# Two-layer hybrid block (S5, DeltaNet, attention) on one core: convolution taps and weight splits moved from ScalarE and GpSimd to VectorE

## The chip, the cores and the metric

The kernel runs on one core of a Trainium2 chip. A core has TensorE (PE, with its weight loads shown as PEld), VectorE (DVE), ScalarE (ACT), GpSimd (POOL) and SyncE (SP), each working through its own queue of instructions in order; an instruction that waits holds everything behind it in its queue. The metric is the device time of one execution in microseconds (us), the median of a few runs.

## The reference, cut to what matters

Two layers over 512 latent tokens and 256 context tokens, model width 1024. In each layer the modulated, normalised input `h` goes through one input projection whose columns feed three token mixers: the bidirectional S5 scan (`u`), the gated DeltaNet (`dq`, `dk`, `dv`, `dz`), and windowed attention (`aq`, `ak`, `av`), beside the merge gates:

```python
(u, dq, dk, dv, dz, db, da, aq, ak, av, gates) = split_cols(h @ w_in, IN_SPLITS)
...
qkv = jnp.concatenate([q, k, v], axis=-1)
qkv = lax.conv_general_dilated(qkv, conv_w[:, None, :].astype(qkv.dtype), window_strides=(1,),
                               padding=[(DN_CONV // 2, DN_CONV // 2)],
                               dimension_numbers=('NWC', 'WIO', 'NWC'),
                               feature_group_count=qkv.shape[-1])
qkv = jax.nn.silu(qkv.astype(jnp.float32))
```

The convolution is depthwise over tokens with 5 taps (`DN_CONV = 5`) on 1536 channels. The first layer also puts out the context stream; the second does not, so there some work is on the 512 latent tokens alone.

## The kernel before, in words

Features lie on the 128 partitions and tokens along the free dimension. Every projection goes by weight tiles of 128 output features: `load_w` fetches a 128x1024 tile (`ws`, three buffers), ScalarE casts it to a high part `wh` (L230), and the engine `g.wle` subtracts to get the low part `wl` (L231); `wh` and `wl` have two buffers each. PE then multiplies three products of high and low parts (`gemm_h`, L180) into a PSUM tile `pg`, of which there are two. `g.wle` is VectorE, except between L1381 and the lines that set it back (L1472 in the first layer, L1514 in the second), the mixer part of a layer, where it is GpSimd.

For each of the 12 feature tiles of the convolution (`conv`, L1398) the PSUM result is copied by ScalarE into a padded tile `cxp` (L943, L945), whose pads GpSimd clears (L942). ScalarE makes tap 0 into `cac` (L949). A tap `j` of 1 to 4 with `j < dve` is one multiply-and-add on VectorE (L952); any other is a ScalarE multiply into a tile `ctp` (L955) and a GpSimd addition into `cac` (L956). The tables `CDV0` and `CDV1` (L1534, L1535) give `dve` for each tile of the first and second layer. ScalarE's tanh (L957) and four VectorE products (L964) finish the tile in `ctp`, and `put` sends it to memory. `cxp`, `cac` and `ctp` have two buffers each. A tile has 772 columns with context and 512 without; in the second layer tiles 0 to 3 (queries) have 512.

While the convolutions run, VectorE also holds the S5 scan, `s5_in` (L649): a recurrence of many steps of four operations each (`mac`, L706 to L709, 384 columns at first, 64 in its later part), and a tail that adds carried state (L729 to L732, 112 to 448 columns). `s5_out` (L736) reads the state on PE (L755 and L757 in the first layer, L762 and L767 in the second, with tables `gm` loaded from memory).

The second layer's program order is `ORD1`: convolutions 4 to 11, 0 to 3, then the attention's keys and values, its queries, then `dn_ba` (L977, L984), then the S5 read-out, attention heads, gates and the DeltaNet main part. The Tile framework's scheduler orders the instructions of each engine from dependencies and its own model of durations, so an edit of one instruction can move others in every engine's queue.

Of the kernel before, what the change touches and what calls it, by code (L numbers as in the profile page):

```python
# [8 lines left out]
F32 = mybir.dt.float32  # L9
# [3 lines left out]
OP = mybir.AluOpType  # L13
# [203 lines left out]
def load_raw(g, src, n=1):  # L217
    t = g.wp.tile([128, 1024], F32, name="ws", tag="ws", bufs=3)
    with paced(g.ldp, g.tc):
        g.wl_last = g.nc.sync.dma_start(t, src).ins  # L220
    return t


def load_w(g, l, i, pool=None):
    nc = g.nc
    s = load_raw(g, g.A["wt"][l, i])
    pool, bufs = (g.wp, 2) if pool is None else (pool, 6)
    hi = pool.tile([128, 1024], F32R, name="wh", tag="wh", bufs=bufs)
    lo = pool.tile([128, 1024], F32R, name="wl", tag="wl", bufs=bufs)
    nc.scalar.copy(hi, s)  # L230
    g.wle.tensor_tensor(lo, s, hi.bitcast(F32), op=OP.subtract)  # L231
    return hi, lo


# [54 lines left out]
def drain(it, n=1):  # L289
    for _ in range(n):  # L290
        next(it, None)
# [642 lines left out]
CW = TOK + 4  # L934
CPAD = TOK + 8


def dn_conv(g, l, pool, i, pl, pc, out_cb, dve):
    nc = g.nc
    xp = pool.tile([128, CPAD], F32, name="cxp", tag="cxp", bufs=2)  # L940
    for a in (0, 2 + LAT, CPAD - 2):
        nc.gpsimd.memset(xp[:, a:a + (4 if a == 2 + LAT else 2)], 0.0)  # L942
    nc.scalar.copy(xp[:, 2:2 + LAT], pl)  # L943
    if pc is not None:
        nc.scalar.copy(xp[:, 6 + LAT:6 + TOK], pc)  # L945
    w = CW if pc is not None else LAT
    cv = g.sm[:, SM_CV + 60 * l + 5 * i:SM_CV + 60 * l + 5 * i + 5]
    acc = pool.tile([128, CW], F32, name="cac", tag="cac", bufs=2)
    nc.scalar.mul(acc[:, :w], xp[:, 0:w], cv[:, 0:1])  # L949
    for j in range(1, 5):  # L950
        if j < dve:
            nc.vector.scalar_tensor_tensor(acc[:, :w], xp[:, j:j + w], cv[:, j:j + 1], acc[:, :w], op0=OP.mult, op1=OP.add)  # L952
        else:
            tap = pool.tile([128, CW], F32, name="ctp", tag="ctp", bufs=2)
            nc.scalar.mul(tap[:, :w], xp[:, j:j + w], cv[:, j:j + 1])  # L955
            nc.gpsimd.tensor_tensor(acc[:, :w], acc[:, :w], tap[:, :w], op=OP.add)  # L956
    nc.scalar.activation(xp[:, :w], acc[:, :w], AF.Tanh, scale=0.5)  # L957
    n = TOK if pc is not None else LAT
    o = pool.tile([128, CW], F32, name="ctp", tag="ctp", bufs=2)[:, :TOK]
    o3 = o.rearrange("p (c i) -> p c i", i=64)  # L960
    for a, m, dst in ((0, 4, o3[:, 0:8:2]), (256, 4, o3[:, 7::-2]), (LAT + 4, 2, o3[:, 8:12:2]), (LAT + 132, 2, o3[:, 11:8:-2])):
        if a < LAT or pc is not None:
            s_ = lambda t: t[:, a:a + 64 * m].rearrange("p (c i) -> p c i", i=64)
            nc.vector.scalar_tensor_tensor(dst, s_(xp), 1.0, s_(acc), op0=OP.add, op1=OP.mult)  # L964
    out_cb(i, o[:, :n])
# [394 lines left out]
def mixers(g, l, hp):  # L1360
    g.marks = {}
    nc, tc, A = g.nc, g.tc, g.A
# [14 lines left out]
    for m in range(4):  # L1377
        w = load_w(g, l, W_U + m)
        for s in both:
            s5_u(g, p5a, ud, u4, m, gemm_h(g, w, s, tag=UT[l] if s == "c" else "g"), s)  # L1380
    g.wle = nc.gpsimd  # L1381

    def s5_start():
        p5b_ = tc.tile_pool(name=f"s5b{l}", bufs=1, reuse_waits="tile")
# [10 lines left out]
    def put(i, acc):  # L1395
        dma(g, QC).dma_start(cvd[i][:, :acc.shape[1]], acc)

    def conv(i, pc, dve=5):  # L1398
        w = load_w(g, l, W_DQ + i)
        pl = gemm_h(g, w, "l")  # L1400
        pcx = gemm_h(g, w, "c") if (cx or i >= 4) else None
        dn_conv(g, l, pc, i, pl, pcx, put, dve)

    def att_kv():
        w = load_w(g, l, W_AK)
# [35 lines left out]
    if cx:  # L1441
# [7 lines left out]
        with tc.tile_pool(name=f"a1{l}", bufs=1, side="right", reuse_waits="tile") as a1:  # L1449
            att_setup(g, l, pa, pa, a1, cx)  # L1450
            ad = adaln(g, 0, range(4, 12), a1, AD1)
            drain(ad)
            att_kv()
            for x, i in enumerate(list(range(4, 12)) + list(range(4))):
                conv(i, a1, CDV0[x])
                drain(ad)
                if x in HS:
                    with tc.issue_after(g.wl_last) if HI else nullcontext():
                        g.hst.pop(0)()
            bat = dn_ba(g, l, a1)  # L1460
# [8 lines left out]
            drain(so, 17)  # L1469
        pa_.__exit__(None, None, None)  # L1470
        s5_close()
        g.wle = nc.vector  # L1472

        def fill(wh):
            if wh == "out":
                place(g, gt, G0, H0, sum(GU0.values()))
# [4 lines left out]
    else:  # L1481
# [3 lines left out]
        a1 = a1_.__enter__()  # L1485
        p5b_, omi, so = s5_start()
        att_setup(g, l, pa, a1, a1, cx)
        qs, x = [None] * 4, 0
        for e in ORD1.split():
            if e == "kv":  # L1490
                att_kv()
            elif e[0] == "q":
                qs[int(e[1])] = att_qt(int(e[1]))
            else:
                conv(int(e), a1, CDV1[x])
                x += 1
        bat = dn_ba(g, l, a1)
        a1_.__exit__(None, None, None)
# [12 lines left out]
        drain(so)  # L1511
        drain(un, N_PRE)
        s5_close()
        g.wle = nc.vector  # L1514

        def fill(wh):
            if wh == "pair":
                drain(un, N_PAIR)
# [12 lines left out]
T0A = 4  # L1531
AD0 = 7
AD1 = 3
CDV0 = [3, 3, 2, 3, 3, 2, 3, 3, 5, 3, 2, 3]  # L1534
CDV1 = [4, 5, 4, 5, 2, 2, 2, 2, 3, 3, 3, 3]  # L1535
ORD1 = "4 5 6 7 8 9 10 11 0 1 2 3 kv q0 q1 q2 q3"
SO0 = 12
SN0 = 2
# [281 lines left out]
def hybrid_block(ctx, tc, A, out):  # L1820
    nc = tc.nc
    g = Ctx()
    g.tc, g.nc, g.A, g.es = tc, nc, A, ctx
    g.tb, g.hd, g.rside, g.pbs, g.plan, g.ldp, g.hst = {}, {}, "right", [], [], [], []
    g.wle = nc.vector
    setup(g)
    s5a_open(g, 0)
    cond_setup(g)
# [76 lines left out]
```

## Time and profile before

| what | value |
|---|---|
| runs | 2878.09, 2886.13, 2887.59 us; median 2886.13 |
| profiled execution | 2888.32 us, span 2886.6 us |
| PE, DVE, ACT, POOL busy | 92%, 58%, 31%, 21% of the span |

Busy shares are means over a span whose stages have different limits. The convolutions of the first layer lie at about 198 to 344 us and those of the second at about 1808 to 1941 us; the rest of each layer's mixers follows them, and the projections and the MLP of a layer lie behind that.

### The profile page before, as it was taken

The page shows a single profiled execution, that of the slowest core. Times are in us where ns is not written, and L with a number is a line of the kernel's source. Part 1 is how long each engine was busy: PE and PEld are TensorE (multiplying, and loading weights), DVE is VectorE, ACT ScalarE, POOL GpSimd, SP SyncE. Part 2 cuts the span into 40 slices and gives each one's busy share as a digit, 9 for nine tenths or more (in the row PEclk, how much of TensorE's full clock was granted, in tenths as well). Part 3 has the DMA queues.
Part 4 walks back from the last instruction along what each step waited for, and adds up shares of the span by engine and source line. Part 5 has one row for each costly group of instructions (what it writes and reads, how often), then busy time and mean ns, then how long its engine had stood idle before and what let it go on. Part 6 is the DMA issues. An engine that isn't in the chain of part 4 may idle for free.

```text
span 2886.6 us, 45481 instructions
## 1 busy us (share of the span) xinstructions
PE 2669.2 (92%) x17644; PEld 2187.7 (76%) x17644; DVE 1669.0 (58%) x4015; ACT 909.1 (31%) x1641; POOL 612.2 (21%) x774
## 2 busy tenths in 40 slices
PE   4698899999999899999999999759997999999998
PEld 1575688878777788788788878647775768889997
DVE  7859763237335665999933324994466368444443
ACT  2343443133222333213131324333342234323322
POOL 5644521021112311000000011562142133100001
PEclk8799997599999999999999999879998999999999
DMA  7665322224315442576421125124433226222232
GB/s 235 177 204 181 136 77 79 69 103 145 91 41 174 139 152 74 163 229 192 119 68 62 65 90 165 64 82 135 134 116 86 99 84 204 93 95 95 88 103 66
DMA packets 206760, 344.62 MB, mean 119 GB/s; under 512 B 89296, under 2 KB 121168, under 8 KB 206416
## 3 DMA queue, kind: packets, MB, share of 16 engines
q1 hardware_dynamic: 171856, 298.61, 32.6%
q0 software_dynamic: 9600, 36.71, 3.8%
q10 hardware_dynamic: 25088, 6.40, 1.0%
q8 instruction: 139, 2.28, 0.3%
q14 instruction: 77, 0.63, 0.1%
HBM read 270.09 MB, written 68.16 MB: 117 GB/s over the span
## 4 chain that ended last, share of the span: by engine, by line
PE 73%; DVE 14%; issue 4%; DMA 4%; POOL 2%; ACT 2%; SPq 1%; ACTq 0%; DVEq 0%; POOLq 0%
PE pg L180 51%; PE pg L1636 4%; PE ps L757 2%; DVE cac L952 2%; PE ps L917 1%; PE ps L906 1%; PE pm L1259 1%; PE pm L1290 1%; DVE st L709 1%; PE pm L1268 1%; PE pg L1686 1%; PE pm L874 1%; PE ps L1305 1%; DVE wl L231 1%; ACT wh L230 1%
## 5 line engine op out<-in xcount | busy, mean ns | idle before, releaser
L230 ACT CAST wh<-ws 128x1024 fp32r<-128x1024 f32 x272 | 285.1, 1049 | 601.6 <-PE pg L180 465.9
L231 DVE TENSOR_TENSOR wl<-ws,wh 128x1024 fp32r<-128x1024 f32 x234 | 293.6, 1256 | 279.7 <-ACT wh L230 275.5
L180 PE MATMUL pg<-hhil,wh 128*128 128x512 f32 x720 | 296.4, 412 | 39.2 <-ACT cxp L943 38.3
L180 PE MATMUL pg<-hhil,wl 128*128 128x512 f32 x720 | 291.7, 405 | 2.2 <-DVE wl L231 2.2
L180 PE MATMUL pg<-hhi,wh 128*128 128x256 f32 (+1 forms) x800 | 280.1, 350 | 14.7 <-ACT cxp L943 13.4
L180 PE MATMUL pg<-hlol,wh 128*128 128x512 f32 x720 | 293.0, 407 | 0.0
L180 PE MATMUL pg<-hh,wh 128*128 128x512 f32 (+1 forms) x832 | 286.3, 346 | 7.2 <-DVE x L1733 6.5
L180 PE MATMUL pg<-hh,wl 128*128 128x512 f32 (+1 forms) x832 | 285.3, 344 | 1.0 <-DVE wl L231 1.0
L180 PE MATMUL pg<-hl,wh 128*128 128x512 f32 (+1 forms) x832 | 285.2, 343 | 0.5 <-DVE hl L1349 0.5
L180 PE MATMUL pg<-hlo,wh 128*128 128x256 f32 (+1 forms) x800 | 279.0, 349 | 1.7 <-DVE hlo L390 1.7
L180 PE MATMUL pg<-hhi,wl 128*128 128x256 f32 (+1 forms) x800 | 276.9, 346 | 0.0
L180 PEld LDWEIGHTS pg<-hhil,wh 128*128 128x128 f32 x720 | 139.3, 194 | 76.3 <-ACT cxp L943 39.7
L180 PEld LDWEIGHTS pg<-hhi,wh 128*128 128x128 f32 x800 | 152.6, 191 | 44.7 <-ACT cxp L943 16.4
L180 PEld LDWEIGHTS pg<-hh,wh 128*128 128x128 f32 x832 | 157.6, 190 | 29.8 <-DVE x L1733 6.4
L1733 DVE SCALAR_TENSOR_TENSOR x<-pg,modv,x 128x512 f32<-128x512 f32 (+1 forms) x104 | 64.7, 626 | 196.8 <-PE pg L180 196.4
L180 PEld LDWEIGHTS pg<-hh,wl 128*128 128x128 f32 x832 | 157.8, 190 | 25.5 <-issue 4.7
L180 PEld LDWEIGHTS pg<-hlo,wh 128*128 128x128 f32 x800 | 152.7, 191 | 31.4 <-issue 12.6
L180 PEld LDWEIGHTS pg<-hl,wh 128*128 128x128 f32 x832 | 157.8, 190 | 22.2 <-issue 4.1
L180 PEld LDWEIGHTS pg<-hhi,wl 128*128 128x128 f32 x800 | 152.8, 191 | 26.7 <-issue 10.5
L180 PEld LDWEIGHTS pg<-hhil,wl 128*128 128x128 f32 x720 | 138.9, 193 | 38.6 <-issue 4.4
L180 PEld LDWEIGHTS pg<-hlol,wh 128*128 128x128 f32 x720 | 139.5, 194 | 32.2 <-issue 3.1
L231 POOL TENSOR_TENSOR wl<-ws,wh 128x1024 fp32r<-128x1024 f32 x38 | 104.6, 2753 | 119.8 <-ACT wh L230 119.7
(463 smaller groups left out, 6033.2 us busy)
## 6 DMA issues: line engine op xcount, KB each, us to landing
ws<-in_wt SPq DMA_DIRECT2D x272, 512.0 KB, 3.6
wa<-in_wmod SPq DMA_DIRECT2D x48, 512.0 KB, 4.9
wa<-in_wmodt SPq DMA_DIRECT2D x48, 512.0 KB, 4.3
gtd<-gr POOLq DMA_DIRECT2D x24, 384.0 KB, 2.9
tg<-gtd POOLq DMA_DIRECT2D x24, 384.0 KB, 3.4
tb<-tC SPq DMA_DIRECT2D x64, 128.0 KB, 2.8
cvd<-ctp SPq DMA_DIRECT2D x20, 384.0 KB, 2.6
gtd<-gr POOLq DMA_DIRECT2D x24, 256.0 KB, 2.6
```

The costliest lines, as they stand in the source:

```text
L180: g.nc.tensor.matmul(ps, lhsT=wt[:, a], rhs=x(k), start=i == 0, stop=i == n - 1)
L230: nc.scalar.copy(hi, s)
L231: g.wle.tensor_tensor(lo, s, hi.bitcast(F32), op=OP.subtract)
L709: v.tensor_tensor(o, t[0], t[1], op=OP.add)
L757: nc.tensor.matmul(o, lhsT=gm[pp, k * 128:k * 128 + 128], rhs=st[pp, k % 2, k // 2, c0:, pr], start=False, stop=k == 3)
L874: nc.tensor.matmul(o, lhsT=q[:, kv, ns], rhs=a.kh[:, kv, ks], start=True, stop=False)
L906: nc.tensor.transpose(p[:, x * 128:x * 128 + 128], Ps[kv][:, i * 128:i * 128 + 128], g.ident)
L917: mi = nc.tensor.matmul(po[64 * kv:64 * kv + 64, :128], lhsT=a.v[:, kt, 64 * kv:64 * kv + 64], rhs=PT[:, 2 * i + kv, :], start=i == 0, sto ...
L952: nc.vector.scalar_tensor_tensor(acc[:, :w], xp[:, j:j + w], cv[:, j:j + 1], acc[:, :w], op0=OP.mult, op1=OP.add)
L1259: nc.tensor.matmul(pk[pps[d], cx(i)], lhsT=kq(h, 0, ch[d]), rhs=S[x][:, d, i], start=True, stop=True, tile_position=(0, 64 * hd[d]))
L1636: nc.tensor.matmul(ps, lhsT=wt[:, a], rhs=x[:, k, sl], start=i == 0, stop=i == 11)
L1733: g.nc.vector.scalar_tensor_tensor(g.x[:, m, sl], acc, g.modv[:, l, 40 + m, p.r:p.r + 1], g.x[:, m, sl], op0=OP.mult, op1=OP.add)
```

## The change

Every tap 1 to 4 becomes a multiply-and-add on VectorE, so the 47 ScalarE multiplies into `ctp` (L955) and 47 GpSimd additions (L956) are gone; 39 of the taps have 772 columns and 8 have 512. The low part of a weight tile is always made on VectorE, which moves 38 of the subtractions there from GpSimd. No other instruction is added or removed.

```diff
@@ -228,7 +228,7 @@
     hi = pool.tile([128, 1024], F32R, name="wh", tag="wh", bufs=bufs)
     lo = pool.tile([128, 1024], F32R, name="wl", tag="wl", bufs=bufs)
     nc.scalar.copy(hi, s)
-    g.wle.tensor_tensor(lo, s, hi.bitcast(F32), op=OP.subtract)
+    nc.vector.tensor_tensor(lo, s, hi.bitcast(F32), op=OP.subtract)
     return hi, lo
 
 
@@ -935,7 +935,7 @@
 CPAD = TOK + 8
 
 
-def dn_conv(g, l, pool, i, pl, pc, out_cb, dve):
+def dn_conv(g, l, pool, i, pl, pc, out_cb):
     nc = g.nc
     xp = pool.tile([128, CPAD], F32, name="cxp", tag="cxp", bufs=2)
     for a in (0, 2 + LAT, CPAD - 2):
@@ -948,12 +948,7 @@
     acc = pool.tile([128, CW], F32, name="cac", tag="cac", bufs=2)
     nc.scalar.mul(acc[:, :w], xp[:, 0:w], cv[:, 0:1])
     for j in range(1, 5):
-        if j < dve:
-            nc.vector.scalar_tensor_tensor(acc[:, :w], xp[:, j:j + w], cv[:, j:j + 1], acc[:, :w], op0=OP.mult, op1=OP.add)
-        else:
-            tap = pool.tile([128, CW], F32, name="ctp", tag="ctp", bufs=2)
-            nc.scalar.mul(tap[:, :w], xp[:, j:j + w], cv[:, j:j + 1])
-            nc.gpsimd.tensor_tensor(acc[:, :w], acc[:, :w], tap[:, :w], op=OP.add)
+        nc.vector.scalar_tensor_tensor(acc[:, :w], xp[:, j:j + w], cv[:, j:j + 1], acc[:, :w], op0=OP.mult, op1=OP.add)
     nc.scalar.activation(xp[:, :w], acc[:, :w], AF.Tanh, scale=0.5)
     n = TOK if pc is not None else LAT
     o = pool.tile([128, CW], F32, name="ctp", tag="ctp", bufs=2)[:, :TOK]
@@ -1378,7 +1373,6 @@
         w = load_w(g, l, W_U + m)
         for s in both:
             s5_u(g, p5a, ud, u4, m, gemm_h(g, w, s, tag=UT[l] if s == "c" else "g"), s)
-    g.wle = nc.gpsimd
 
     def s5_start():
         p5b_ = tc.tile_pool(name=f"s5b{l}", bufs=1, reuse_waits="tile")
@@ -1395,11 +1389,11 @@
     def put(i, acc):
         dma(g, QC).dma_start(cvd[i][:, :acc.shape[1]], acc)
 
-    def conv(i, pc, dve=5):
+    def conv(i, pc):
         w = load_w(g, l, W_DQ + i)
         pl = gemm_h(g, w, "l")
         pcx = gemm_h(g, w, "c") if (cx or i >= 4) else None
-        dn_conv(g, l, pc, i, pl, pcx, put, dve)
+        dn_conv(g, l, pc, i, pl, pcx, put)
 
     def att_kv():
         w = load_w(g, l, W_AK)
@@ -1452,7 +1446,7 @@
             drain(ad)
             att_kv()
             for x, i in enumerate(list(range(4, 12)) + list(range(4))):
-                conv(i, a1, CDV0[x])
+                conv(i, a1)
                 drain(ad)
                 if x in HS:
                     with tc.issue_after(g.wl_last) if HI else nullcontext():
@@ -1469,8 +1463,7 @@
             drain(so, 17)
         pa_.__exit__(None, None, None)
         s5_close()
-        g.wle = nc.vector
-
+    
         def fill(wh):
             if wh == "out":
                 place(g, gt, G0, H0, sum(GU0.values()))
@@ -1492,7 +1485,7 @@
             elif e[0] == "q":
                 qs[int(e[1])] = att_qt(int(e[1]))
             else:
-                conv(int(e), a1, CDV1[x])
+                conv(int(e), a1)
                 x += 1
         bat = dn_ba(g, l, a1)
         a1_.__exit__(None, None, None)
@@ -1511,8 +1504,7 @@
         drain(so)
         drain(un, N_PRE)
         s5_close()
-        g.wle = nc.vector
-
+    
         def fill(wh):
             if wh == "pair":
                 drain(un, N_PAIR)
@@ -1531,8 +1523,6 @@
 T0A = 4
 AD0 = 7
 AD1 = 3
-CDV0 = [3, 3, 2, 3, 3, 2, 3, 3, 5, 3, 2, 3]
-CDV1 = [4, 5, 4, 5, 2, 2, 2, 2, 3, 3, 3, 3]
 ORD1 = "4 5 6 7 8 9 10 11 0 1 2 3 kv q0 q1 q2 q3"
 SO0 = 12
 SN0 = 2
@@ -1822,7 +1812,6 @@
     g = Ctx()
     g.tc, g.nc, g.A, g.es = tc, nc, A, ctx
     g.tb, g.hd, g.rside, g.pbs, g.plan, g.ldp, g.hst = {}, {}, "right", [], [], [], []
-    g.wle = nc.vector
     setup(g)
     s5a_open(g, 0)
     cond_setup(g)
```

Because the scheduler orders each queue, the edit moves other instructions too. Three places are shown. Rows name the line of the respective file, so L952 of before is L951 of the changed kernel, and L964 is L959.

The first is on DVE in the second layer, at the end of the last convolution. Before:

```order
L732 TENSOR_TENSOR st<-scs 128x3x7x16
L732 TENSOR_TENSOR st<-scr 128x7x16
L952 SCALAR_TENSOR_TENSOR cac<-cxp,sm,cac 128x512
L729 TENSOR_TENSOR scs<-st,apw_16612 128x112
L730 TENSOR_TENSOR scs<-st,apw_16612 128x112
L952 SCALAR_TENSOR_TENSOR cac<-cxp,sm,cac 128x512
L731 TENSOR_TENSOR scs<-scs,st 128x112
L964 SCALAR_TENSOR_TENSOR ctp<-cxp,cac 128x4x64 x2
L732 TENSOR_TENSOR st<-scs 128x7x16
L964 SCALAR_TENSOR_TENSOR ctp<-cxp,cac 128x4x64 x2
L808 STREAM_SHUFFLE ash<-arf 128x512
```

The last rows of the S5 tail (L729 to L732) stand among the last taps, and the last L964 is followed by attention work (L808) alone. In the changed kernel, the same place around the last L959:

```order
L951 SCALAR_TENSOR_TENSOR cac<-cxp,sm,cac 128x512
L708 TENSOR_TENSOR scr<-scr,st 128x64
L951 SCALAR_TENSOR_TENSOR cac<-cxp,sm,cac 128x512
L709 TENSOR_TENSOR st<-scr 128x2x2x16
L231 TENSOR_TENSOR wl<-ws,wh 128x1024
L706 TENSOR_TENSOR scs<-st,apw_16562 128x64
L707 TENSOR_TENSOR scs<-st,apw_16562 128x64
L959 SCALAR_TENSOR_TENSOR ctp<-cxp,cac 128x4x64 x2
L808 STREAM_SHUFFLE ash<-arf 128x512
L708 TENSOR_TENSOR scs<-scs,st 128x64
L810 TENSOR_TENSOR ash<-ash,rt 128x512
L709 TENSOR_TENSOR st<-scs 128x2x2x16
```

Here the 64-column recurrence is still under way at the last convolution's end. The first rows of the S5 tail in the changed kernel come some twenty rows behind that:

```order
L729 TENSOR_TENSOR scr<-st,apw_16562 128x448
L730 TENSOR_TENSOR scr<-st,apw_16562 128x448
L708 TENSOR_TENSOR scs<-scs,st 128x64
L731 TENSOR_TENSOR scr<-scr,st 128x448
L709 TENSOR_TENSOR st<-scs 128x2x2x16
L732 TENSOR_TENSOR st<-scr 128x4x112
```

All 24 operations with 448 columns, 24 with 336 and 8 with 112 of the tail, and 18 operations with 64 columns of the recurrence, stand behind the last L959; before, none stood behind the last L964.

The second place is on PE in the second layer, where the first read-out of the S5 state stands (L767). Before:

```order
L180 MATMUL pg<-hhic,wh 128x256
L180 MATMUL pg<-hloc,wh 128x256
L180 MATMUL pg<-hhic,wl 128x256
L767 MATMUL ps<-gm,st 64x128 x8
L762 MATMUL ps<-mt,u_16357 64x128 x2
L767 MATMUL ps<-gm,st 64x128 x8
L762 MATMUL ps<-mt,u_16357 64x128
L180 MATMUL pg<-hhil,wh 128x512
L180 MATMUL pg<-hlol,wh 128x512
```

L767 comes right behind the context part of the value projection (L180 with 256 columns). In the changed kernel:

```order
L180 MATMUL pg<-hhil,wh 128x512
L180 MATMUL pg<-hlol,wh 128x512
L180 MATMUL pg<-hhil,wl 128x512
L874 MATMUL pm<-akh,aq 128x384
L875 MATMUL pm<-akl,aq 128x384
L874 MATMUL pm<-akh,aq 128x384
L767 MATMUL ps<-gm,st 64x128 x8
L762 MATMUL ps<-mt,u_16307 64x128 x2
L767 MATMUL ps<-gm,st 64x128 x8
L762 MATMUL ps<-mt,u_16307 64x128 x2
L767 MATMUL ps<-gm,st 64x128 x8
```

It now comes behind the four query projections, `dn_ba`, the first gate projections (57 more matmuls of 512 columns of the gates than stood ahead of the DeltaNet main part before) and the first attention products (L874): 537 matmuls of 512 columns of the projections stand between the layer's S5 input (L685) and it, where 312 stood before.

The third is on DVE in the first layer, during the convolutions; before:

```order
L706 TENSOR_TENSOR scs<-st,apw_1338 128x384
L707 TENSOR_TENSOR scs<-st,apw_1338 128x384
L952 SCALAR_TENSOR_TENSOR cac<-cxp,sm,cac 128x772
L709 TENSOR_TENSOR st<-scr 128x2x12x16
L708 TENSOR_TENSOR scs<-scs,st 128x384
L952 SCALAR_TENSOR_TENSOR cac<-cxp,sm,cac 128x772
L706 TENSOR_TENSOR scr<-st,apw_1338 128x384
L707 TENSOR_TENSOR scr<-st,apw_1338 128x384
L262 TENSOR_REDUCE md<-ps 128x8
L709 TENSOR_TENSOR st<-scs 128x2x12x16
```

and in the changed kernel at the same place:

```order
L951 SCALAR_TENSOR_TENSOR cac<-cxp,sm,cac 128x772
L706 TENSOR_TENSOR scs<-st,apw_1338 128x384
L707 TENSOR_TENSOR scs<-st,apw_1338 128x384
L709 TENSOR_TENSOR st<-scr 128x2x12x16
L951 SCALAR_TENSOR_TENSOR cac<-cxp,sm,cac 128x772
L708 TENSOR_TENSOR scs<-scs,st 128x384
L231 TENSOR_TENSOR wl<-ws,wh 128x1024
L706 TENSOR_TENSOR scr<-st,apw_1338 128x384
L707 TENSOR_TENSOR scr<-st,apw_1338 128x384
L709 TENSOR_TENSOR st<-scs 128x2x12x16
L951 SCALAR_TENSOR_TENSOR cac<-cxp,sm,cac 128x772
```

The four taps of a tile, and a weight's low part (L231), now stand in one queue with the recurrence.

## Rows read from the trace of the kernel before

**Rows 1.** The page: busy time, share and instructions of each engine.

```profile
PE 2669.2 (92%) x17644; PEld 2187.7 (76%) x17644; DVE 1669.0 (58%) x4015; ACT 909.1 (31%) x1641; POOL 612.2 (21%) x774
```

**Rows 2.** Windows: start:end length, busy (count) PE PEld DVE ACT POOL, PEclk, DMA, GB/s.

```profile
198.00:328.00 130.00, 112.36 (x587) 76.40 (x584) 128.07 (x221) 48.50 (x68) 69.45 (x50) 0.95 0.52 184
...
1808.00:1943.00 135.00, 87.51 (x386) 71.44 (x385) 130.76 (x206) 49.23 (x66) 81.59 (x55) 0.82 0.20 67
1943.00:2010.00 67.00, 62.52 (x411) 47.75 (x413) 29.95 (x55) 23.01 (x39) 17.93 (x14) 0.92 0.48 143
2010.00:2086.00 76.00, 76.00 (x518) 58.93 (x515) 29.07 (x91) 25.57 (x43) 8.90 (x19) 1.00 0.45 145
2086.00:2222.00 136.00, 122.77 (x1007) 98.11 (x1006) 99.71 (x347) 56.58 (x131) 46.61 (x88) 0.92 0.37 102
```

**Rows 3.** PE's waits in 198 to 345: line, releaser, us, times, longest.

```profile
PE pg L180 <- ACT cxp L943: 13.4, 6, 5.5
```

**Rows 4.** PE's waits in 1808 to 1955.

```profile
PE pg L180 <- ACT cxp L943: 43.4, 6, 13.1
PE ps L767 <- DMA gm<-tb: 8.5, 1, 8.5
```

**Rows 5.** DVE timeline, 211 to 222: start, duration (us).

```profile
214.05 0.55 DVE L708 TENSOR_TENSOR scr<-scr,st 128x384 f32<-128x384 f32 x1
214.51 2.20 DVE L706 TENSOR_TENSOR scs<-st,apw 128x384 f32<-128x384 f32 x1
```

**Rows 6.** POOL timeline, 205 to 222; the last row holds three additions.

```profile
214.27 6.21 POOL L956 TENSOR_TENSOR cac<-cac,ctp 128x772 f32<-128x772 f32 x3 [0.85 <-DVE cac L952]
```

**Rows 7.** DVE timelines, 244 to 252 and 1904 to 1912.

```profile
247.72 1.01 DVE L952 SCALAR_TENSOR_TENSOR cac<-cxp,sm,cac 128x772 f32<-128x772 f32 x1
248.66 0.55 DVE L708 TENSOR_TENSOR scs<-scs,st 128x384 f32<-128x384 f32 x1
...
1907.72 0.74 DVE L952 SCALAR_TENSOR_TENSOR cac<-cxp,sm,cac 128x512 f32<-128x512 f32 x1
```

**Rows 8.** DVE groups by shape, 198 to 328: count, busy us, mean ns, idle before.

```profile
L952 DVE SCALAR_TENSOR_TENSOR cac<-cxp,sm,cac 128x772 f32<-128x772 f32 x17 | 23.6, 1387 | 0.0
L264 DVE TENSOR_TENSOR modv<-md,sm 128x8 f32<-128x8 f32 x7 | 8.2, 1174 | 0.0
```

**Rows 9.** DVE groups by shape, 1808 to 1943.

```profile
L952 DVE SCALAR_TENSOR_TENSOR cac<-cxp,sm,cac 128x772 f32<-128x772 f32 x11 | 15.8, 1440 | 3.6 <-ACT cac L949 3.6
L952 DVE SCALAR_TENSOR_TENSOR cac<-cxp,sm,cac 128x512 f32<-128x512 f32 x8 | 11.2, 1396 | 0.0
...
L732 DVE TENSOR_TENSOR st<-scs 128x448 f32<-128x448 f32 x3 | 1.8, 615 | 0.0
...
L707 DVE TENSOR_TENSOR scs<-st,apw 128x64 f32<-128x64 f32 x6 | 1.3, 217 | 0.0
```

**Rows 10.** POOL groups by shape, 198 to 328.

```profile
L956 POOL TENSOR_TENSOR cac<-cac,ctp 128x772 f32<-128x772 f32 x18 | 43.4, 2409 | 20.0 <-DVE cac L952 14.4 <-ACT wh L230 1.5 <-ACT ctp L955 1.1
L231 POOL TENSOR_TENSOR wl<-ws,wh 128x1024 fp32r<-128x1024 f32 x8 | 25.7, 3207 | 8.3 <-ACT wh L230 8.3
```

**Rows 11.** POOL groups by shape, 1808 to 1943.

```profile
L956 POOL TENSOR_TENSOR cac<-cac,ctp 128x772 f32<-128x772 f32 x13 | 33.6, 2584 | 10.8 <-issue 5.2 <-ACT ctp L955 4.4 <-DVE cac L952 0.9
L231 POOL TENSOR_TENSOR wl<-ws,wh 128x1024 fp32r<-128x1024 f32 x11 | 33.2, 3017 | 16.9 <-ACT wh L230 16.8
L956 POOL TENSOR_TENSOR cac<-cac,ctp 128x512 f32<-128x512 f32 x7 | 14.2, 2026 | 6.7 <-DVE cac L952 4.0 <-ACT ctp L955 2.7
```

**Rows 12.** The page, costliest groups: the weight split on each engine.

```profile
L231 DVE TENSOR_TENSOR wl<-ws,wh 128x1024 fp32r<-128x1024 f32 x234 | 293.6, 1256 | 279.7 <-ACT wh L230 275.5
...
L231 POOL TENSOR_TENSOR wl<-ws,wh 128x1024 fp32r<-128x1024 f32 x38 | 104.6, 2753 | 119.8 <-ACT wh L230 119.7
```

**Rows 13.** PE timeline, 2070 to 2072: start, duration (us).

```profile
2070.14 0.39 PE L180 MATMUL pg<-hlol,wh 128*128 128x512 f32 x1
2070.37 0.39 PE L180 MATMUL pg<-hhil,wl 128*128 128x512 f32 x1
```

## The prediction

> **What bounds the kernel now.** I read the page's busy shares first. PE is busy 92% of the span and DVE 58% [rows 1], so over the whole kernel PE is the bound and little can be gained except where PE starves. The windows by stage say where that is. In the first layer's convolutions, 198 to 328 us, DVE is busy 128.07 of 130 us and PE 112.36; in the second layer's, 1808 to 1943, DVE is busy 130.76 of 135 us and PE only 87.51, at a granted clock of 0.82 [rows 2]. The next two stages are PE's (62.52 of 67 and 76.00 of 76, DVE at 29.95 and 29.07), and the DeltaNet stage from 2086 lies between (PE 122.77 of 136, DVE 99.71) [rows 2]. PE's waits name what is late: its gemms wait for ACT's copy of PSUM into `cxp`, 13.4 us in the first layer and 43.4 us in the second [rows 3, 4]. That copy waits for a `cxp` buffer, which DVE's last products of an earlier tile free. So both stages hang on DVE's queue, and an edit there is worth what it takes from that queue, until PE's own work ends later.
>
> **What DVE's time is made of.** The timeline shows a two-input operation of 128x384 at 0.55 us when alone, and the same shape at 2.20 us while GpSimd runs its additions L956 at 214.27 to 220.48 [rows 5, 6]. A 772-column tap takes 1.01 us alone, a 512-column one 0.74 [rows 7], yet their means in the stages are 1387, 1440 and 1396 ns, and L264, with 8 columns, averages 1174 [rows 8, 9]. I call the excess over the lone duration a stall. For the taps it is 17 x (1.387 - 1.01) = 6.4 us in the first stage, and 11 x 0.43 + 8 x 0.656 = 4.7 + 5.2 = 9.9 us in the second. The same subtraction over every form of the two DVE views gives 44 and 48 us. A check: GpSimd spends 43.4 + 25.7 = 69.1 us of the first stage and 33.6 + 33.2 + 14.2 = 81.0 us of the second in additions and splits [rows 10, 11], so a stall of 44 and 48 is 0.6 of that time, and cannot be more than all of it.
>
> The Trainium skill (SBUF — State Buffer, section Who interferes with whom) says that a DVE instruction with two SBUF inputs and a GpSimd instruction that reads SBUF share one port pair under an exclusive lock, so that the loser fully blocks. Rows 5 and 6 agree as to the pairing; by a full block throughout, the stall would be all of 69.1 and 81.0 us, and the measured excess is less.
>
> **The change, part by part.**
>
> *GpSimd's additions and splits go.* In the two stages nothing of GpSimd is left but memsets of 0.1 us or so. The stalls of 44 and 48 us go with them. Bounds: nothing (if the stretch had another cause) and 69.1 and 81.0 us. I take 44 and 48, worked out from this kernel's own durations.
>
> *DVE gets taps and splits.* Consecutive DVE operations overlap, so a tap costs the distance to the next start: 248.66 - 247.72 = 0.94 us for 772 columns, and with the same 0.07 off, 0.67 for 512 [rows 7]. A split on DVE has a mean of 1256 ns over 234 of them [rows 12]; less the same overlap and some stalls, 1.14. First stage: 18 taps and 8 splits [rows 10], 18 x 0.94 + 8 x 1.14 = 26 us. Second: 13 and 7 taps and 11 splits [rows 11], 12.2 + 4.7 + 12.5 = 29 us. DVE's queue gets shorter by 44 - 26 = 18 and 48 - 29 = 19 us. If every added operation still had its stretched price, about 1.4 us a tap and, in the same ratio, 1.7 a split, the added cost would be 39 and 47, and the net 5 and 1.
>
> *ACT loses 47 multiplies.* ACT is busy 48.50 of 130 and 49.23 of 135 us [rows 2]; that time was never the bound, but a tap no longer passes through two other engines. I cost this at nothing, for DVE's full queue covers it.
>
> *The order on DVE in the second layer.* As the rows of the order show, all of the S5 tail and 18 steps of the recurrence move behind the last convolution's last product. At lone durations this is 24 x 0.615 for 448 columns, 18 x 0.217 for 64 [rows 9], and between them in proportion 24 x 0.50 for 336 and 8 x 0.27 for 112: 32.8 us, less 0.07 of overlap for each of 74 operations: 27.5 us. It is not saved, but put beside the kv, query and gate gemms, where DVE has 37 and 47 us free in 67 and 76 [rows 2]. So the last convolution ends 19 + 27 = 46 us earlier, bounded by PE's floor there: 87.51 x 0.82 = 72 us at full clock against 135 - 46 = 89. PE's 43.4 us of waits [rows 4] are what is bought, with 8.5 of the wait for `gm`, which is late only because the read-out stands early.
>
> *What is given back.* PE's read-out now stands behind 57 more gate matmuls. At the step of PE for 512 columns, 2070.37 - 2070.14 = 0.23 us [rows 13], they make 13.3 us of work that filled before the DeltaNet stage, where PE already idles 136 - 122.77 = 13.2 us [rows 2]. That stage's DVE (99.71 of 136) may then have nothing for PE to do beside it. Between nothing and 13 given back, and as DVE's moved tail also competes with the attention's DVE work, I take 10: second layer 46 - 10 = 36 us.
>
> *First layer.* DVE's 18 us meets PE's floor: PE idles only 130 - 112.36 = 17.6 us there [rows 2], and 13.4 of that is the wait that goes [rows 3]. DVE's need falls to 128 - 18 = 110, PE's stays at 112.4: two near-equal chains that feed each other through two PSUM tiles do not both run full. I take 12, between 0 and 17.6. The order of PE behind the convolutions stays as it was.
>
> Other splits of the 38 lie in the attention stages where DVE has slack, and are costed at nothing; without that cover they would be 19 x 1.14 = 22 us.
>
> **Sum.** 12 + 36 = 48 us from the profiled execution's 2888.3, so 2840; that execution is 2.2 above the median of the runs, so 2838 for the median. Changes under 0.3% (8.7 us) can't be told from none.
>
> **The rivals.**
>
> *Only the stalls count.* If the moved S5 tail makes the read-out, the heads or the DeltaNet stage late by as much as the convolutions gained, 27 is lost: 12 + 19 = 31, or 19 alone if PE holds the first stage. 2855 to 2867. For it: S5's end gates L767, and PE waited for tables there [rows 4]. Against: PE's order has 537 - 312 = 225 more gemm matmuls ahead of that point, which at 0.23 us is 52 us of cover.
>
> *More than that.* If nothing is given back and the first stage gains PE's whole 17.6: 17.6 + 46 = 64, so 2822; and with the granted clock of the DeltaNet stage rising from 0.92 to the 1.00 of the stage before it [rows 2], 122.77 x 0.08 = 10 more: 2812.
>
> *No change.* First layer 0 (PE's floor), second 46 - 27 - 13 = 6: 2880. It needs all give-backs at once.
>
> *Slower: the splits hold DVE's queue.* GpSimd's splits waited 119.7 us in all for ACT's cast [rows 12], a wait that there stopped only later additions. In DVE's in-order queue the recurrence and the taps stand behind the split, as the third place of the order shows; a wait there stops everything. At all of it, 120 - 48 = 72 us slower, 2958; it decides against my forecast from 48 us of such waits. Against: in the two saturated stages it was only 8.3 and 16.8 us [rows 10, 11], and the scheduler puts a split where it expects the cast to be done. DVE's 234 splits show such waits too (279.7 us idle [rows 12]), but in stages with DVE slack.
>
> *Slower: the stretch was not GpSimd's.* Then DVE, busy 98% and 97%, gets 26 + 29 = 55 us more: 2941. Rows 5 and 6 speak against it.
>
> The Trainium skill (Perfetto Trace Analysis, section Optimizing Scalar/DVE Operations) speaks against this change: where DVE is saturated, moving work off it to ScalarE or even GpSimd may make sense, and the change does the reverse. It adds that GpSimd and DVE share an SBUF read port, so that moving work between those two might not help, which rows 5 and 6 bear out.
>
> **Chances.** Forecast (2822 to 2854) 0.66; more than that 0.05; stalls only 0.15; no change 0.06; splits in the queue 0.05; stretch not GpSimd's 0.03. Faster: 0.66 + 0.05 + 0.15 = 0.86 and a little of the no-change case, 0.87; same 0.05; slower 0.08. The range 2812 to 2870 takes in the first three cases.
>
> **What would show it.** In the profile after, two-input DVE operations in the convolution stages should have their lone durations (taps near 1.0 and 0.74, L706 at 0.55 us); PE's wait for `cxp` in the second layer should fall from 43.4 to under 15 us and the clock there rise above 0.82; the last convolution should end near 1941 - 12 - 46 = 1883 us; the tail L729 to L732 should run beside kv and query gemms. It is wrong if DVE shows waits for the cast of tens of us in these stages, if L767 or the heads wait for L732, or if PE's idle time in the DeltaNet stage grows by over 13 us.

## The result and the profile after

The changed kernel takes 2806.76 us (median of 4 runs, 2803.78 to 2808.68), the kernel before 2882.66 (4 runs, 2878.09 to 2887.59): the ratio is 0.974, with a 95% interval of 0.9724 to 0.9756, so 70 to 80 us faster. The forecast was 2838, with a range of 2812 to 2870, so the time lies 5 us below the range. The direction and the mechanism held; the gain of 76 us was sized at 48.

The page's line of busy times, which answers to [rows 1]:

```profile
span 2806.9 us, 45417 instructions
PE 2642.2 (94%) x17644; PEld 2171.5 (77%) x17644; DVE 1643.6 (59%) x4100; ACT 871.0 (31%) x1594; POOL 402.5 (14%) x689
```

The span is 79.7 us shorter (2886.6 - 2806.9). PE runs the same 17644 matmuls, but is busy for 27.0 us less (2669.2 - 2642.2) and idle for 52.7 less. DVE has 85 more instructions, the 47 taps and 38 splits, and yet is busy for 25 us less. This is the first thing to see: more work, less time on the engine that got it.

The DVE groups by shape of the changed kernel, first in 198 to 323 us (first layer's convolutions), then in 1780 to 1868 (second layer's), answer to [rows 8, 9]:

```profile
L951 DVE SCALAR_TENSOR_TENSOR cac<-cxp,sm,cac 128x772 f32<-128x772 f32 x42 | 42.5, 1015 | 0.2 <-issue 0.2
L231 DVE TENSOR_TENSOR wl<-ws,wh 128x1024 fp32r<-128x1024 f32 x10 | 12.2, 1223 | 7.4 <-ACT wh L230 7.3
...
L706 DVE TENSOR_TENSOR scs<-st,apw 128x384 f32<-128x384 f32 x7 | 3.8, 550 | 0.0
...
L951 DVE SCALAR_TENSOR_TENSOR cac<-cxp,sm,cac 128x512 f32<-128x512 f32 x16 | 11.7, 744 | 0.0
```

Taps are at 1015 and 744 ns, where before they averaged 1387 to 1440 and 1396; the recurrence is at 550 ns. These are the lone durations of [rows 5, 7]. The splits' waits for the cast, the fear of one rival, are 7.3 us here and 2.5 in the second layer.

Windows over the same two stages and two later ones (columns as in [rows 2]):

```profile
198.00:323.00 125.00, 123.56 (x706) 87.29 (x705) 111.39 (x239) 42.51 (x61) 1.54 (x27) 1.00 0.57 198
...
1780.00:1868.00 88.00, 78.78 (x393) 64.95 (x392) 85.36 (x168) 33.33 (x48) 1.82 (x25) 0.96 0.29 98
1868.00:2010.00 142.00, 138.10 (x890) 105.49 (x889) 84.39 (x172) 48.12 (x78) 16.78 (x28) 1.00 0.49 160
2010.00:2140.00 130.00, 115.37 (x839) 91.13 (x839) 101.59 (x388) 55.25 (x131) 44.83 (x87) 0.93 0.33 91
```

In the first layer PE is now busy for 123.56 of 125 us at a clock of 1.00. In the second, the convolutions take 88 us instead of 135, with DVE still full (85.36) and the clock at 0.96 instead of 0.82. PE's waits there, which answer to [rows 4]:

```profile
PE pg L180 <- ACT cxp L943: 7.2, 4, 2.8
PE pg L977 <- ACT arf L807: 2.2, 1, 2.2
```

The 43.4 us have become 7.2. In the first layer no wait for `cxp` L943 is left.

To count the gain, both kernels are cut at the same matmuls: the end of the S5 input of a layer, the start of the first layer's read-out, and the start of the merge in the second. Windows of before, then of after:

```profile
197.00:468.30 271.30, 246.34 (x1524) 188.28 (x1524) 212.00 (x439) 114.36 (x203) 118.83 (x129) 0.96 0.39 132
...
1807.10:2361.40 554.30, 480.34 (x3573) 373.61 (x3572) 350.40 (x872) 191.28 (x362) 184.17 (x238) 0.92 0.31 97
```

```profile
195.70:446.70 251.00, 239.68 (x1530) 186.34 (x1528) 195.94 (x476) 97.20 (x181) 29.50 (x92) 0.99 0.43 143
...
1778.30:2281.90 503.60, 468.44 (x3574) 364.02 (x3572) 333.32 (x907) 174.93 (x342) 92.13 (x203) 0.96 0.34 106
```

With the same number of matmuls to within 6 the first stretch is 20.3 us shorter and the second 50.7. In the first, PE's idle time fell from 24.96 to 11.32 (-13.6) and its busy time by 6.7; in the second, idle fell from 74.0 to 35.2 (-38.8), busy by 11.9. The other 8.7 of the 79.7 us lie outside these stretches. Part of them is scatter: the profiled execution of before, 2888.32 us, was 5.7 above its median, that of the changed kernel, 2808.68, only 1.9.

### The profile page after: what moved, and what is told of

It is laid out like the page before. It is cut to its first block, busy times and chain, and to the rows that moved or that the text cites. A ratio compares the mean times of both kernels' runs of the same rounds, so it can differ in the third digit from the quotient of the medians.

```text
span 2806.9 us, 45417 instructions
## 1 busy us (share of the span) xinstructions
PE 2642.2 (94%) x17644; PEld 2171.5 (77%) x17644; DVE 1643.6 (59%) x4100; ACT 871.0 (31%) x1594; POOL 402.5 (14%) x689
## 5 line engine op out<-in xcount | busy, mean ns | idle before, releaser
L231 DVE TENSOR_TENSOR wl<-ws,wh 128x1024 fp32r<-128x1024 f32 x272 | 340.7, 1254 | 299.5 <-ACT wh L230 286.9
L180 PE MATMUL pg<-hhil,wh 128*128 128x512 f32 x720 | 292.6, 407 | 10.6 <-ACT cxp L943 7.2
L180 PE MATMUL pg<-hh,wh 128*128 128x512 f32 (+1 forms) x832 | 287.2, 347 | 6.5 <-DVE x L1723 3.0
L180 PE MATMUL pg<-hhil,wl 128*128 128x512 f32 x720 | 289.6, 403 | 2.6 <-DVE wl L231 2.6
L180 PE MATMUL pg<-hlol,wh 128*128 128x512 f32 x720 | 289.7, 403 | 0.0
L180 PE MATMUL pg<-hh,wl 128*128 128x512 f32 (+1 forms) x832 | 285.9, 344 | 1.0 <-DVE wl L231 1.0
L180 PE MATMUL pg<-hl,wh 128*128 128x512 f32 (+1 forms) x832 | 286.6, 345 | 0.0
L180 PE MATMUL pg<-hhi,wh 128*128 128x256 f32 (+1 forms) x800 | 278.4, 348 | 2.7 <-ACT arf L807 1.5
L180 PE MATMUL pg<-hlo,wh 128*128 128x256 f32 (+1 forms) x800 | 277.8, 347 | 1.7 <-DVE hlo L390 1.7
L180 PE MATMUL pg<-hhi,wl 128*128 128x256 f32 (+1 forms) x800 | 276.1, 345 | 0.0
L180 PEld LDWEIGHTS pg<-hh,wh 128*128 128x128 f32 x832 | 158.5, 191 | 29.3 <-issue 6.7
L180 PEld LDWEIGHTS pg<-hhi,wh 128*128 128x128 f32 x800 | 152.5, 191 | 34.0 <-issue 12.4
L180 PEld LDWEIGHTS pg<-hh,wl 128*128 128x128 f32 x832 | 158.9, 191 | 23.9 <-issue 3.3
L180 PEld LDWEIGHTS pg<-hlo,wh 128*128 128x128 f32 x800 | 152.1, 190 | 30.4 <-issue 11.4
L180 PEld LDWEIGHTS pg<-hl,wh 128*128 128x128 f32 x832 | 158.9, 191 | 21.5 <-issue 4.3
L180 PEld LDWEIGHTS pg<-hhil,wh 128*128 128x128 f32 x720 | 137.5, 191 | 44.9 <-ACT cxp L943 8.2
L180 PEld LDWEIGHTS pg<-hhi,wl 128*128 128x128 f32 x800 | 152.3, 190 | 24.2 <-issue 8.3
L180 PEld LDWEIGHTS pg<-hhil,wl 128*128 128x128 f32 x720 | 137.2, 191 | 38.8 <-DVE wl L231 3.9
L180 PEld LDWEIGHTS pg<-hlol,wh 128*128 128x128 f32 x720 | 137.5, 191 | 33.2 <-issue 3.9
L1626 PE MATMUL pg<-yh,wh 128*128 128x512 f32 (+1 forms) x288 | 105.2, 366 | 11.0 <-DVE macc L1629 6.1
```

What stands on the lines that cost most here:

```text
L180: g.nc.tensor.matmul(ps, lhsT=wt[:, a], rhs=x(k), start=i == 0, stop=i == n - 1)
L231: nc.vector.tensor_tensor(lo, s, hi.bitcast(F32), op=OP.subtract)
L1626: nc.tensor.matmul(ps, lhsT=wt[:, a], rhs=x[:, k, sl], start=i == 0, stop=i == 11)
```

## The experiments

**One part alone.** Two kernels split the change by what moves:

```diff
-CDV0 = [3, 3, 2, 3, 3, 2, 3, 3, 5, 3, 2, 3]
-CDV1 = [4, 5, 4, 5, 2, 2, 2, 2, 3, 3, 3, 3]
+CDV0 = [5] * 12
+CDV1 = [5] * 12
```

> Only the taps move to DVE; the 38 weight splits stay on GpSimd. Theory A (GpSimd's operations on SBUF stretch DVE's two-input operations while DVE is full): overlaps in the trace of before put 25.8 and 27.3 us of DVE's stretch beside the additions, against 17 and 17 us of added taps, so this part has about 19 of the 35 us of net DVE relief and should give about 42 of the 76 us: 2841 us; DVE operations beside the splits stay stretched. Theory B (a tap that passes ACT and GpSimd makes each tile late, the splits don't matter): nearly all of it, about 2812 us.

```diff
-    g.wle = nc.gpsimd
+    g.wle = nc.vector
```

> Only the 38 weight splits move to DVE; the taps stay divided as before. Theory A: 17.2 and 20.0 us of stretch go, 9 and 12.5 us of DVE work come, about 16 of 35 us of net relief, so about 34 us faster: 2849 us. Theory B: no change within 8 us, or slower by the splits' waits in DVE's queue (8 and 17 us).

Taps alone: 2823.86 us, ratio 0.9797 (0.9779 to 0.9816), 58 us faster. Splits alone: 2845.13 us, 0.987 (0.9851 to 0.989), 37 us faster. Theory B by itself falls with the splits: no tap's path was shortened there, and 37 us came. Theory A has the signs, but its shares were too small, above all for the taps (42 expected), and the two parts overlap: 58 + 37 = 95, where both together give 76. The order on DVE is a likely reason. With the taps alone, all 56 operations of the second layer's S5 tail already stand behind the last convolution's last product, as in the changed kernel; with the splits alone, 30 of the 56 do; before, none. So both runs hold a share of the order's gain, and neither measures the stretch alone. The stretch itself was only partly gone: with either part alone, a tap is still stretched by what is left on GpSimd. In the second layer's convolutions, with only the taps moved, and then with only the splits moved:

```profile
L952 DVE SCALAR_TENSOR_TENSOR cac<-cxp,sm,cac 128x772 f32<-128x772 f32 x24 | 36.8, 1542 | 0.0
L952 DVE SCALAR_TENSOR_TENSOR cac<-cxp,sm,cac 128x512 f32<-128x512 f32 x16 | 16.1, 1011 | 0.0
```

```profile
L952 DVE SCALAR_TENSOR_TENSOR cac<-cxp,sm,cac 128x772 f32<-128x772 f32 x11 | 16.8, 1530 | 3.6 <-ACT cac L949 3.6
```

**One layer alone.** Both parts, with the other layer's table and split engine as before.

```diff
-CDV0 = [3, 3, 2, 3, 3, 2, 3, 3, 5, 3, 2, 3]
+CDV0 = [5] * 12
...
-    g.wle = nc.gpsimd
+    g.wle = nc.vector if cx else nc.gpsimd
```

> Both parts, in the first layer alone. From the two traces the first layer gained 23 us by the start of its merge, where the forecast's term said 12. If the layers add up, 2883 - 23 = 2860 us. If the first layer's gain is what the second layer's or the run-to-run scatter lent it, 2871 us (the term of 12).

The other kernel does the same with `CDV1` and the two engines exchanged:

> Both parts, in the second layer alone. From the two traces the second layer gained 51 us, where the forecast said 46 less 10 given back in the DeltaNet stage. If nothing is given back: 2832 us. If 10 is given back there and the rest of the 76 has another source: 2847 us.

First layer: 2862.94 us, 0.9929 (0.9913 to 0.9944), so 16 to 25 us, 19 by the medians. Second: 2834.81 us, 0.9836 (0.9817 to 0.9854), 42 to 53 us, 48 by the medians. The forecast's 12 and 36 lie below both intervals. The two add up to 67 of the 76 us, which the intervals allow.

**GpSimd busy without a use.** To the changed kernel as many GpSimd operations were added beside the convolutions as there had been additions, on a scratch tile that nothing reads:

```diff
+    with g.tc.issue_after(pad):
+        junk = pool.tile([128, 720], F32, name="junk", tag="junk", bufs=1)
+        nc.gpsimd.memset(junk[:, :nj], 0.0)
+        for _ in range(5 - (CDV0[(i - 4) % 12] if l == 0 else CDV1[(i - 4) % 12])):
+            nc.gpsimd.tensor_tensor(junk[:, :nj], junk[:, :nj], junk[:, :nj], op=OP.add)
```

> The changed kernel, with 47 more GpSimd additions of a scratch tile to itself (720 or 512 columns) beside the convolutions, as many for each tile as the kernel before had, and a memset of that tile; nothing reads the result and nothing waits for it but GpSimd's next pads. Theory A (GpSimd's reading of SBUF stretches DVE): DVE's two-input operations beside them are stretched again, up to the 53 us that the trace of before shows beside its additions, and the time is about 2840 us (2825 to 2860). Theory B (the hops between engines were the cost): no hop comes back, 2807 within 8 us.

In the second kernel each addition is three memsets, and nothing else differs:

> As the kernel with the added additions, but each is three memsets of the same scratch tile, so that GpSimd is busy for about as long and writes SBUF without reading it. Theory A: no stretch, 2807 us within 8. Rival (any busy GpSimd stretches DVE): as the additions do, about 2840 us.

With additions 2835.71 us (2834.18 to 2839.1), 29 us slower than the changed kernel; with memsets 2807.98 (2805.7 to 2810.75), no change. First-layer groups of the kernel with additions, DVE and then GpSimd:

```profile
L961 DVE SCALAR_TENSOR_TENSOR cac<-cxp,sm,cac 128x772 f32<-128x772 f32 x41 | 49.3, 1206 | 0.3 <-issue 0.2
...
L708 DVE TENSOR_TENSOR scr<-scr,st 128x384 f32<-128x384 f32 x7 | 5.0, 718 | 0.0
...
L952 POOL TENSOR_TENSOR junk<-junk 128x720 f32<-128x720 f32 x18 | 36.3, 2019 | 1.4
```

And of the kernel with memsets:

```profile
L962 DVE SCALAR_TENSOR_TENSOR cac<-cxp,sm,cac 128x772 f32<-128x772 f32 x42 | 42.6, 1017 | 0.2 <-issue 0.2
...
L709 DVE TENSOR_TENSOR st<-scr 128x384 f32<-128x384 f32 x7 | 3.9, 552 | 0.0
...
L953 POOL MEMSET junk<- 128x720 f32 x55 | 38.5, 701 | 3.2
```

GpSimd is busy for 36.3 us in the one and 38.5 in the other. Only the GpSimd operations that read SBUF stretch DVE: 1206 against 1017 ns for a tap, 718 against 552 for the recurrence. In both kernels the second layer's S5 tail stands behind the last product, as in the changed kernel, so the order is not what differs. This shows theory A for 29 us: with the memsets GpSimd is as busy and has the same hops to the other engines, and no time is lost. Whether the way of a tap through ScalarE and GpSimd had a part of its own in the 58 us of the taps was not tested. The Trainium skill (SBUF — State Buffer, section Who interferes with whom) says that a DVE instruction with two SBUF inputs contends with a GpSimd instruction that reads SBUF and not with one that only writes it; both runs agree.

**The moved S5 tail.** In the changed kernel, the last convolution of the second layer was put back behind the tail on DVE:

```diff
-        dn_conv(g, l, pc, i, pl, pcx, put)
+        with nullcontext() if cx or i != 3 else tc.issue_after(g.s5_last):
+            dn_conv(g, l, pc, i, pl, pcx, put)
```

> The changed kernel, with one constraint: in the second layer the last convolution's DVE operations are queued behind the last operation of the S5 tail, as they stood before the change; nothing else is added. If the moved tail is worth the forecast's 27 us: 2807 + 27 = 2834 us. Rival (PE has other gemms by then, and the last convolution's end sets nothing): within 8 us of 2807.

It takes 2831.45 us (2828.11 to 2836.07), 25 us of the 27 expected. This constraint is close to the order of before, but not the same: before, 52 of the 56 tail operations started ahead of the last convolution's first tap on DVE, mixed with the taps of the three tiles ahead of it; here those tiles are done first, and the whole tail stands ahead of all four taps of the last. And the wait on PE is not at a convolution. PE's waits from the end of the S5 input:

```profile
PE ps L767 <- DMA gm<-tb: 33.7, 1, 33.7
PE pg L180 <- ACT cxp L943: 7.2, 4, 2.8
```

The wait for `cxp` L943 stays at 7.2; the loss shows as one wait at the read-out, whose table loads into the buffer (`tbr`) that the tail uses as scratch, and in this kernel's order the read-out stands ahead of the query projections again. So a run was made that also puts the read-out behind them:

```diff
+        with tc.issue_after(g.ba_last):
+            for _ in range(16):
+                drain(so)
```

> As order_back (the S5 tail ahead of the last convolution on DVE), with one more constraint: PE's S5 read-out stands behind the query projections and the beta and decay projection, about where the changed kernel has it. In order_back PE stood 33.7 us at the read-out, waiting for a table that loads into the buffer of the tail's scratch. If the read-out's place on PE was what cost: within 8 us of 2807. If the last convolution's place on DVE cost: 2831 stays.

2829.37 us (2824.16 to 2829.85): at most a few us better, although the wait at L767 is gone. By the ratios to the kernel before, 0.9829 (0.9814 to 0.9844) for the first constraint and 0.9804 (0.9789 to 0.9818) for both, against 0.974, they cost 26 and 18 us.

```profile
PE pg L180 <- ACT arf L807: 33.5, 1, 33.5
PE pg L180 <- ACT cxp L943: 8.0, 5, 2.1
```

The wait has moved to the next projection, whose PSUM tile ACT had not yet copied into `arf` (L807). ACT's timeline of this kernel shows what held ACT:

```profile
1859.58 1.04 ACT L230 CAST wh<-ws 128x1024 fp32r<-128x1024 f32 x1 [2.55 <-PE pg L180]
1891.94 0.63 ACT L952 ACTIVATE cxp<-cac 128x512 f32<-128x512 f32 x1 [31.32 <-DVE cac L951]
1892.48 0.58 ACT L807 ACTIVATE arf<-pg 128x512 f32<-128x512 f32 x1
```

The tanh of the last convolution (L952) waits 31.32 us for its last tap on DVE, and in ACT's queue the copy that would free PSUM for PE stands right behind it. The kernel with the read-out early has the same wait on ACT (31.3 us) beside PE's own at the table. So the second alternative holds: it is the last convolution's place on DVE that costs. With the read-out late it reaches PE by ACT's queue; with the read-out early, PE meets the wait for the table first.

In the kernel before, this wait on ACT was not there. In 1900 to 1960 us its tanh (L957 there) never waited longer than 3.0 us for a tap:

```profile
ACT cxp L957 <- POOL cac L956: 11.8, 5, 3.0
```

There the tail was spread over the last four tiles, and PE's waits were those of [rows 4], at `cxp` above all. The two runs thus show what the tail costs when it stands ahead of the last convolution, about what the forecast's term said, but not the way that it took before.

The same constraint on the read-out alone, in the kernel before:

> The kernel before with that one constraint on PE alone: the second layer's read-out behind the query projections. If only the 8.5 us that PE waited for the table there can be won: 2882 - 8 = 2874 us. If the read-out's place was worth the forecast's 27 us by itself: 2855 us.

2875.68 us, ratio 0.9982 (0.9964 to 1.0): between 10 us and nothing. PE's waits:

```profile
PE pg L180 <- ACT cxp L943: 43.6, 7, 13.0
PE pg L180 <- ACT arf L807: 7.5, 1, 7.5
```

The 8.5 us at the table became 7.5 at `arf`. The read-out's place on PE is worth little by itself.

**Further in the same direction.** The first layer's S5 output tables are the last large block of GpSimd reads beside a full DVE:

```diff
-T0P = [('c', 0), ('c', 1)]
+T0P = []
```

> The changed kernel with the last large GpSimd work beside a full DVE moved as well: the first layer's S5 output tables (about 60 us on GpSimd between 40 and 120 us, where DVE is busy 79 of 80 us and shows 34 us of stretch) are made on DVE. Theory A by the same sum: 34 us of stretch go, about 50 operations of 512 columns at 0.67 us come, so nothing net, but the tables are needed only at the read-out, so urgent work is no longer held: 0 to 20 us faster than 2807. Rival: DVE is already full up to 323 us, the added 34 us come out of that, 10 to 30 us slower.

2776.24 us (2768.66 to 2778.32), ratio to the kernel before 0.9631 (0.9614 to 0.9649): 30 us better than the changed kernel, more than I expected. Windows of 40 to 120 us, of the changed kernel and then of this one:

```profile
40.00:120.00 80.00, 42.88 (x260) 28.12 (x260) 78.84 (x127) 26.17 (x59) 58.60 (x55) 0.73 0.54 160
```

```profile
40.00:120.00 80.00, 65.70 (x423) 49.36 (x423) 79.32 (x196) 31.55 (x68) 3.25 (x3) 0.83 0.79 247
```

DVE is full in both, but gets through 196 operations instead of 127, and PE through 423 matmuls instead of 260. Of the 69 more on DVE, 52 are the ones that GpSimd no longer does there (55 and 3). The stretch is gone; one form of the tables, before and after this step:

```profile
L563 DVE TENSOR_TENSOR tux<-tB,apw 128x448 f32<-128x448 f32 x28 | 23.9, 910 | 0.0
```

```profile
L563 DVE TENSOR_TENSOR tux<-tB,apw 128x448 f32<-128x448 f32 x24 | 13.5, 616 | 0.0
```

By the sum that stood ahead of this run, stretch and added work cancel. Why 30 us came, and not 0 to 20, is not shown.

Then GpSimd's additions and products of the merge stage were moved as well, where DVE is not full:

```diff
-                    e = nc.gpsimd if bi == 1 else nc.vector
-                    e.tensor_tensor(macc[:, m, sl], macc[:, m, sl], tg[:, sl], op=OP.add)
+                    nc.vector.tensor_tensor(macc[:, m, sl], macc[:, m, sl], tg[:, sl], op=OP.add)
...
-        nc.gpsimd.tensor_tensor(q, q, y, op=OP.mult)
+        nc.vector.tensor_tensor(q, q, y, op=OP.mult)
```

> The kernel with the S5 tables on DVE, and with GpSimd's 24 additions and 8 products of the merge stage made on DVE too. There DVE is not full (93 of 136 us in the first layer's merge, 74 of 87 in the second's), and 13 us of stretch stand beside GpSimd's work. If a stretch costs only where DVE is full: within 8 us of 2776. Rival (each us of stretch counts wherever it lies): 13 us less, 24 x 0.5 + 8 x 0.8 = 18 us more work, so a loss, or a gain of the waits for the two engines' hops: anything from 10 us faster to 10 slower.

2771.9 us (2767.26 to 2775.15), ratio 0.9619 (0.96 to 0.9637), which can't be told from the kernel without it; theory and rival both allow the 4 us. This run decides nothing. Beside it the changed kernel was run once more:

> The changed kernel once more, on the chip of the run beside it, so that the versions compare on one chip: 2807 us within 5.

2808.74 us (2801.55 to 2812.51). The version with tables and merge on DVE has the lowest median, 37 us below it.

## Why the prediction was right, and where it was wrong

The time came out 5 us below the range. The mechanism was right, and two terms of the sum were mis-sized: the 10 us given back (none were) and the first layer's 12 us (19 measured). Seen from PE, the sum took its busy time as fixed, and that fell by 18.6 us.

*GpSimd's additions and splits stretch DVE (44 and 48 us): right.* Lone durations came back in both layers, and the pair of runs with additions and memsets shows the cause. The bounds of 69.1 and 81.0 us took it that DVE always loses; GpSimd's splits, 2.41 us in the median, took 6.91 us at 206 us and 5.72 at 1895, so GpSimd was held up as well. That the splits on DVE would hold its queue was a rival rightly priced low (7.3 and 2.5 us). DVE's total fell by 25 us as it took on more. The Trainium skill (Perfetto Trace Analysis, section Optimizing Scalar/DVE Operations) says that relieving a saturated DVE by the other engines may make sense, with a caution about the read port that GpSimd and DVE share; here the caution was the case.

*The order term (27 us in the second layer): about right in size.* Two runs that put the tail back ahead of the last convolution cost 25 and 23 us by the medians (26 and 18 by the ratios). In these runs the loss reaches PE through the read-out's table or, with the read-out late, through the last convolution's tanh, which holds ACT's queue and with it the next projection's PSUM tile; in the kernel before it was the wait at `cxp` that I had in mind, 43.4 us against 7.2 after. Counted from the end of the S5 input (1807.1 and 1778.3 us), the last convolution's last product ends 50 us earlier (at 1945.9 and 1866.8), where 46 had been forecast.

*"Between nothing and 13 given back ... I take 10": wrong, nothing was.* Windows of the DeltaNet stage up to the merge, of before, of the changed kernel, and of the kernel with the tail back:

```profile
2086.00:2361.40 275.40, 253.41 (x2260) 194.68 (x2259) 160.13 (x522) 92.56 (x210) 75.75 (x151) 0.95 0.29 87
```

```profile
2017.30:2281.90 264.60, 242.56 (x2203) 185.38 (x2202) 157.14 (x535) 88.08 (x205) 71.53 (x148) 0.94 0.28 82
```

```profile
2032.50:2303.60 271.10, 252.29 (x2256) 195.26 (x2255) 160.17 (x527) 92.84 (x211) 76.22 (x151) 0.95 0.30 89
```

The 57 gate matmuls did move ahead (2260 to 2203), and the stage became shorter by 10.8 us, nearly the 13.3 that I had priced them at. PE's idle time in it is 22.0 us before, 22.0 after and 18.8 with the tail back. So those matmuls filled at most 3 us of bubbles; I took idle time in a stage as proof that what PE did beside it was filling it. So the second layer gained 48 us in the run of its own and 50.7 by the traces, not 36.

*"PE's stays at 112.4: two near-equal chains ... do not both run full; I take 12": wrong, and the largest miss beside the give-back.* PE does run full beside DVE's chain: PE is busy for 123.56 of 125 us, DVE for 111.39. The first layer gave 19 us by the run of its own and 20.3 up to the read-out by the traces. The floor was mis-set in two ways: the stage that I cut ended at 328, with 4.9 us of idle time behind that (17 - 12.07 in 328 to 345), and PE's 112.36 us were counted as fixed, while they were taken at a clock of 0.95. The order was overlooked here too: in the first layer 24 of the 56 tail operations, 11.3 us by their durations, moved behind the last product, where none had stood. What that is worth by itself was not tested.

*PE's busy time, put at nothing: wrong.* Seen from PE, the 71 us of the two stretches are 13.6 + 38.8 = 52.4 us less idle time and 6.7 + 11.9 = 18.6 us less busy time for the same matmuls, with the granted clock at 0.99 and 0.96 instead of 0.96 and 0.92. This divides the same gain a second way and is not to be added to the misses above. The first layer's term held PE's busy time fixed. A gain by the clock I had given only to the rival "more than that", with a chance of 0.05, and there in the DeltaNet stage, where the clock stayed (0.95 before, 0.94 after). That the idle time alone fell by about the 48 us of the forecast is luck, as the 48 was meant for the whole gain. What sets the clock was not tested by itself: in the kernel with the tail back, PE's idle time in the second stretch is 24 us longer than in the changed one, in one lump for the most part, without more busy time. So the gain in busy time goes with the clock in the convolution stages, and no more is shown.

## What to carry to other kernels

Where DVE is full of two-input operations, price a GpSimd operation that reads SBUF by the stretch that it lays on DVE beside its own time, and compare this with the time of the same operation on DVE. Where the two were close, as for the tables, the move still won here; that the scheduler can then put off what isn't urgent is a reason, seen here only for the S5 tail. An order that the scheduler changes comes with every part of an edit, so look for it in each run before adding the parts up. When PE starves, count what it gets back in idle time and in busy time at the higher clock. PE's idle time in a stage doesn't show that the independent work in it fills bubbles: here, taking 57 matmuls out of the DeltaNet stage made it shorter by nearly their price.

## What the runs showed that was not expected

Three memsets of 0.70 us that only write cost DVE nothing, where an addition of about the same total length (2.02 us) stretched the taps by 19%. With DVE busy 79 of 80 us in both cases, taking about 55 us of GpSimd work onto DVE let it finish 196 operations instead of 127 in the same window, the 52 moved ones and 17 more, and made the kernel 30 us faster: a busy share of 98% says nothing of how much of it is stretch inside instructions. And a wait on PE kept its length, 33.7 and 33.5 us, when the instruction that had shown it was moved away: two waits ran side by side, and the waits view names the one that PE meets first.
